# A hybrid decoder block on one Trainium2 core: the order of seven Strassen products, and 512 columns per matmul in two projections

## The chip, the cores and the metric

The kernel runs on one core of one Trainium2 chip. The metric is the device time of one execution in microseconds (us). The kernel before was run three times: 1019.54, 1021.58 and 1021.25 us, median 1021.25.

## The reference

One layer of a decoder with 512 tokens, model width 1024, all in float32:

```
h    = rmsnorm(x, norm_mix_w)
proj = h @ w_in                  # zs, the SSM's inputs, the GDN's inputs, its gate, gs and gg
y    = ssd_scan(...)             # Mamba-2 mixer, 16 heads of 64, 2 groups
y    = y * silu(zs)              # zs: the SSM's gate, 1024 columns
y    = y * rsqrt(mean(y*y) per group of 512) * ssm_norm_w
y_gdn = gated delta rule mixer (8 heads of 128), with its own gate and norm
merged = sigmoid(gs) * (y @ w_proj_ssm) + sigmoid(gg) * (y_gdn @ w_proj_gdn)
x    = x + merged @ w_out        # the output projection
h    = rmsnorm(x, norm_ffn_w)
gate, up = split(h @ w_ffn_in)   # 2 x 2816 columns
x    = x + (silu(gate) * up) @ w_ffn_down
out  = rmsnorm(x, final_norm_w)
```

## The kernel before

Every large product is done as three matmuls (`three`, L342): each float32 operand is split into a high half, rounded to `fp32r`, and a low half, the rest, also `fp32r`; then high by high, high by low and low by high are added in PSUM. `split` (L265) has ScalarE copy the high half (`whi`) and VectorE subtract it from the source for the low half (`wlo`).

**Weights** come in *units* of 128 partitions x 1024 numbers: SP's queue loads one into a buffer `wst`, ScalarE and VectorE split it into `whi` and `wlo` (three buffers each). `cols` (L338) makes of 1024 x 256 weights two units, each of four 128-row tiles by 256 columns. All jobs stand in one list, and their units in one stream. `unit()` (L331) hands the next unit to a job; `ahead(n_split, n_load)` (L278) splits the next units before they are needed, as many as it is told, and loads some more.

**Order.** The program writes the instructions of TensorE (PE), VectorE (DVE) and ScalarE (ACT) in the order in which each engine then runs them. A planner (`Weave`) makes that order: side work, such as a norm after a product, stands in generators, and `tick()` (L85) sets in, between matmuls, what would be ready by the planner's own costs. `start` (L82) begins such work, and `until` (L104) advances the planner's clock until named events are done.

**Jobs around the change**, with the time at which the profiled execution is there: three of the four `gs` jobs (until 503), four `zs` jobs of 256 columns (L1083, 503 to 551), the last `gs` job (to 563), the SSM projection (`ps_job`, to 607), the output projection (`wo_job`, `wo_last`, to 656), the feed-forward blocks (to 894), and the down projection. The last `gs` job stands behind the zs jobs to give the norm after them time.

`gemm_tm` (L377) makes token-major products: for each of four groups of 128 tokens, the activations are the stationary operand and 256 weight columns stream. It goes over the tokens with the first unit, then with the second, and after each token of the second starts `after(t, ...)`. For the zs jobs this is the gate: Silu on ScalarE out of PSUM (`zs`), the product with the scan's output on VectorE (`xg`), and once a group's 512 columns are there, `ssd_norm` (L1066): a square with a sum on ScalarE (`jk`), small steps on GpSimd, a scaling on VectorE, four transposes on TensorE, and their copy and split (`ysh`, `ysl`).

For the output projection `after` is `wo_residual` (L1140): VectorE adds the residual (`x2`), and after a token's last 256 columns come the square on ScalarE (`hn`), two scalings of 512 columns on VectorE (`hn`), eight transposes, copies, and after every second token the split of the transposed activations `h2w` (`h2_split`, L1155; `h2_sums`, L1161). `wo_job` does the first and second 256 columns, `wo_last` (L1201) the third and fourth, two tokens at a time.

**Feed-forward.** The 2816 hidden columns are taken in 11 blocks of 256 for gate and up. The first (`ffn_first`, L1384) is done plainly, with units `wkeep`. The ten others (`ffn_block`, L1399) use Strassen's scheme: seven products instead of eight of 24 matmuls of 256 columns, on sums of the activations and sums of the weights (b11, b21, t1, t2, t3, b22 and b21 once more as a sum). t1 and t3 are summed by a load with addition on GpSimd's queue; t2 and the second b21 by VectorE (`sums` in `ffn_units`, L1272). Seven products write five PSUM banks: P1 and P2 share A, P7 and P4 share C:

```
ORDER = ("P1", "P2", "P5", "P6", "P7", "P3", "P4")                                          # L1265
BANK = {"P1": "A", "P2": "A", "P5": "D", "P6": "B", "P7": "C", "P3": "F", "P4": "C"}         # L1266
until(("a", name), *{"P2": [("p1", fp)], "P4": [("c22", fp)]}.get(name, []))               # L1403
```

P2 adds onto P1 in bank A, and ScalarE's copy `p1` must take P1 out first; P4 adds onto P7 in bank C, and VectorE's `c22` must read it first. `ffn_post` (L1313) is the work on the banks: the copy `p1`, Silu, `u2`, `w`, `c22` and so on. In the last block VectorE and ScalarE also split the activations for the down projection (`actw`, `act_split`, L1416).

Of the kernel before, what the change touches and what calls it, by code (L numbers as in the profile page):

```python
# [14 lines left out]
P = 128  # L15
T = 512
NT = T // P
# [159 lines left out]
def hybrid_block_kernel(  # L177
# [25 lines left out]
    def psum(s="p"):  # L203
        return ps.tile([P, 512], F32, tag="p", name=nm(s))
# [133 lines left out]
    def cols(w, off):  # L338
        return [(w[kh * 512:(kh + 1) * 512, off:off + 256].rearrange("(k p) c -> p k c", p=P), 4, 256)
                for kh in range(2)]  # L340

    def three(p, a, b, first, last, **kw):  # L342

        te.matmul(p, a[0], b[0], start=first, stop=False, **kw)
        te.matmul(p, a[0], b[1], start=False, stop=False, **kw)
        te.matmul(p, a[1], b[0], start=False, stop=last, **kw)
# [29 lines left out]

    def gemm_tm(hT, tokens, after):  # L377

        hhi, hlo = hT
        out_ = {t: psum("pt")[:, 0:256] for t in tokens}  # L380
        for kh in range(2):
            whi, wlo = unit()
            for t in tokens:
                ts = slice(t * P, (t + 1) * P)
                for kk in range(4):
                    k = 4 * kh + kk
                    three(out_[t], (hhi(k)[:, ts], hlo(k)[:, ts]), (whi[:, kk], wlo[:, kk]),
                          k == 0, k == KT - 1)
                    if kk % 2:
                        tick()  # L390
                if kh:
                    start(after(t, out_[t]))
                if t == tokens[0]:
                    ahead(2, 3)


# [685 lines left out]

    def zs_job(g, q):  # L1083
        if g == 0 and q == 0:
            until(("scan", 0), ("scan", 1))
            mid.bcs = m4([D], s="bcs")
            sy.dma_start(mid.bcs, ssm_norm_w.broadcast_to([P, D]))
            mid.ys = (alloc(2, "ysh"), alloc(2, "ysl"))

        def gate(t, p):  # L1090
            zs = s2([256], "zs")
            ac.activation(zs, p, AF.Silu)
            yield HOP
            yv = xg[g][:, t, 256 * q:256 * q + 256]
            ve.tensor_tensor(yv, yv, zs, ALU.mult)
            if q:
                yield from ssd_norm(g, t)

        gemm_tm(hT, range(NT), gate)

# [31 lines left out]
    for g in range(2):  # L1132
        for q in range(2):
            job(lambda g=g, q=q: zs_job(g, q), *cols(w_in, OFF_ZS + 512 * g + 256 * q))
    job(lambda: gs_job(3), *cols(w_in, OFF_GS + 768))
# [4 lines left out]
    def wo_residual(q, t, p):  # L1140
        xv = mid.x2[t // 2][:, t % 2]
        xq = xv[:, 256 * q:256 * q + 256]
        ve.tensor_tensor(xq, p, xq, ALU.add)
        if q == 3:
            hn = b8([D], s="hn")
            yield from norm_T("h2", t, xv, hn, [mid.bcf[:, 0:512], mid.bcf[:, 512:D]], hn, put_h2(t))
            if t % 2:
                spawn(h2_sums(t // 2), wv.cur)
        yield True
# [40 lines left out]
    def wo_job(q):  # L1190
        if q == 0:
# [6 lines left out]
            until(*[("mg", k) for k in range(KT)])  # L1198
        gemm_tm(parts(*mid.mg), range(NT), lambda t, p: wo_residual(q, t, p))

    def wo_last():  # L1201

        mhi, mlo = parts(*mid.mg)

        def piece(p, t, kh, w):
            ts = slice(t * P, (t + 1) * P)
            for kk in range(4):
                k = 4 * kh + kk
                three(p, (mhi(k)[:, ts], mlo(k)[:, ts]), (w[0][:, kk], w[1][:, kk]), k == 0, k == KT - 1)
                if kk % 2:  # L1210
                    tick()

        pts = [psum("pt")[:, 0:256] for _ in range(NT)]
        w = unit()
        for t in range(NT):
            piece(pts[t], t, 0, w)
            if t == 0:
                ahead(2, 3)
        ahead(2, 3)
        ws = []  # L1220

        def second(t):
            if t == 0:
                ws.append(unit())
            piece(pts[t], t, 1, ws[0])
            start(wo_residual(2, t, pts[t]))

        def third(t):
            p = psum("pt")[:, 0:256]
            for kh in range(2):  # L1230
                if t == 0:
                    ws.append(unit())
                piece(p, t, kh, ws[1 + kh])
                if t == NT - 1 and kh == 0:
                    ahead(2, 3)
            start(wo_residual(3, t, p))

        for t in range(2):
            second(t)
            third(t)  # L1240
        second(2)
        second(3)
        ahead(1, 3)
        third(2)
        third(3)

    for q in range(2):
        job(lambda q=q: wo_job(q), *cols(w_out, 256 * q))
    job(wo_last, *cols(w_out, 512), *cols(w_out, 768))

# [13 lines left out]
    NB = FH // 256  # L1264
    ORDER = ("P1", "P2", "P5", "P6", "P7", "P3", "P4")  # L1265
    BANK = {"P1": "A", "P2": "A", "P5": "D", "P6": "B", "P7": "C", "P3": "F", "P4": "C"}  # L1266
# [5 lines left out]
    def ffn_units(fp):  # L1272
# [27 lines left out]
        def sums():  # L1300
# [4 lines left out]
            (lambda: get("b11", 0, 0), None),  # L1305
            (lambda: get("b21", 1, 0), None),
            (t1, sums),
            (t2, None),
# [229 lines left out]
```

## Time and profile before

| | |
|---|---|
| times of three runs | 1019.54, 1021.58, 1021.25 us (median 1021.25) |
| profiled execution, and its span in the trace | 1021.12 us, 1019.4 us |
| instructions | 15625 |
| TensorE matmuls / weight loads | busy 996.5 / 885.7 us, 6394 each |
| VectorE, ScalarE, GpSimd | busy 630.2, 455.3, 96.1 us |
| HBM | 111 GB/s over the span |

The span is the time from the first to the last instruction that the profiler saw; the rest of the execution's time lies around it. A matmul's record ends after the next one has begun, so that a matmul's cost is read from the distance of two starts. In rows of a timeline the columns are the start and the duration in us, engine, line, operation, output <- inputs, shapes, and how many neighbours are joined; in brackets stand the engine's idle time before the row and what ended it. L164, L168 and L153 are lines of helpers that issue every instruction of an engine, so the tiles' names tell the work: `pw`, `pt`, `pdn` are PSUM tiles, `h2w` the split activations of the feed-forward.

### The profile page before, as it was taken

Reading aid. Unit: us, or ns where it says so; the run is one execution under the profiler, and the core shown is the slowest. Engines: PE = TensorE matmul, PEld = TensorE weight load, DVE = VectorE, ACT = ScalarE, POOL = GpSimd, SP = SyncE. Lnnn points to the kernel's source line nnn. Section 1 sums busy time; section 2 is a strip of 40 time slices with the busy share of each in tenths; the row PEclk is TensorE's granted clock in tenths of the full one; section 3 lists DMA queues with packets and bytes.
Section 4 is the critical chain, followed back from the end, with each engine's and each line's share of the span. In section 5 each row is a group of like instructions: output and inputs, shape, how many; then the busy total and the mean of one; then the engine's idle time right before and its main releaser. Section 6 shows DMA issues by size and latency. Waiting matters only on the chain. (4 is left out here: it accounts for less than half of the span.)

```text
span 1019.4 us, 15625 instructions
## 1 busy us (share of the span) xinstructions
PE 996.5 (98%) x6394; PEld 885.7 (87%) x6394; DVE 630.2 (62%) x914; ACT 455.3 (45%) x831; POOL 96.1 (9%) x124
## 2 busy tenths in 40 slices
PE   7999999999999999999999999999999999999997
PEld 5888878888888888878899889999999999988885
DVE  5676699654576879763145463587777777961422
ACT  5466535467676573112345232554344444642222
POOL 2051001100011030000011000111111111000000
PEclk9999999999999999999999999999999999999999
DMA  6242222221112723243332353267677676333322
GB/s 196 63 168 82 83 84 62 64 83 42 42 51 75 248 82 107 80 112 95 104 84 80 107 166 104 62 166 166 166 174 198 158 173 166 108 120 104 99 67 82
DMA packets 99911, 114.02 MB, mean 112 GB/s; under 512 B 6218, under 2 KB 91367, under 8 KB 99072
## 3 DMA queue, kind: packets, MB, share of 16 engines
q1 hardware_dynamic: 89278, 102.54, 32.5%
q0 software_dynamic: 10560, 10.49, 6.8%
q8 instruction: 50, 0.82, 0.3%
q14 instruction: 21, 0.17, 0.1%
q10 hardware_dynamic: 2, 0.00, 0.0%
HBM read 110.87 MB, written 2.15 MB: 111 GB/s over the span
## 5 line engine op out<-in xcount | busy, mean ns | idle before, releaser
L153 DVE TENSOR_TENSOR wlo<-wst,whi 128x1024 fp32r<-128x1024 f32 x174 | 215.0, 1236 | 224.7 <-ACT whi L153 218.5
L153 ACT CAST whi<-wst 128x1024 fp32r<-128x1024 f32 x174 | 182.1, 1048 | 231.4 <-PE pw L164 125.8
L164 PE MATMUL pw<-h2w,whi 128*128 128x256 f32 x1120 | 203.0, 284 | 7.0 <-ACT p L153 7.0
L164 PE MATMUL pw<-hhi,whi 128*128 128x512 f32 (+1 forms) x496 | 196.7, 397 | 0.8 <-ACT whi L153 0.8
L164 PE MATMUL pw<-hhi,wlo 128*128 128x512 f32 (+1 forms) x496 | 191.1, 385 | 2.3 <-DVE wlo L153 2.3
L164 PE MATMUL pw<-hlo,whi 128*128 128x512 f32 (+1 forms) x496 | 190.6, 384 | 0.0
L164 PEld LDWEIGHTS pw<-h2w,whi 128*128 128x128 f32 x1120 | 174.6, 192 | 9.0 <-ACT p L153 9.0
L164 PE MATMUL pw<-h2w,wlo 128*128 128x256 f32 x560 | 158.4, 283 | 0.0
L164 PEld LDWEIGHTS pw<-hhi,wlo 128*128 128x128 f32 x496 | 93.7, 189 | 21.8 <-DVE wlo L153 2.9
L164 PEld LDWEIGHTS pw<-hhi,whi 128*128 128x128 f32 x496 | 93.8, 189 | 17.4 <-ACT whi L153 1.1
L164 PE MATMUL pdn<-whi,actw 128*128 128x512 f32 x352 | 108.6, 389 | 0.0
L164 PEld LDWEIGHTS pw<-hlo,whi 128*128 128x128 f32 x496 | 94.0, 190 | 16.3
L164 PEld LDWEIGHTS pw<-h2w,wlo 128*128 128x128 f32 x560 | 107.5, 192 | 0.0
L164 PEld LDWEIGHTS pdn<-whi,actw 128*128 128x128 f32 x352 | 66.1, 188 | 13.6
L164 PE MATMUL pdn<-wlo,actw 128*128 128x512 f32 x176 | 68.5, 389 | 0.0
L153 DVE SCALAR_TENSOR_TENSOR acc<-pw,pg,acc 128x511 f32<-128x511 f32 (+2 forms) x72 | 53.6, 746 | 2.8 <-ACT acc L153 0.9
L153 POOL DMA_DIRECT2D wst<-in_w_ffn_in_dram x20 | 25.9, 1296 | 243.0 <-DMA wst<-in_w_ffn_in_dram 143.3
L164 PE MATMUL pw<-yg,whi 128*128 128x512 f32 x128 | 42.9, 416 | 0.0
L164 PEld LDWEIGHTS pdn<-wlo,actw 128*128 128x128 f32 x176 | 33.0, 188 | 6.9
L164 PE MATMUL pt<-whi,hhi 128*128 128x256 f32 x128 | 36.5, 285 | 0.0
L164 PE MATMUL pt<-wlo,mgh 128*128 128x256 f32 x128 | 36.3, 284 | 0.1
L164 PE MATMUL pt<-whi,mgh 128*128 128x256 f32 x128 | 36.4, 284 | 0.0
(269 smaller groups left out, 1545.5 us busy)
## 6 DMA issues: line engine op xcount, KB each, us to landing
wst<-in_w_in_dram SPq DMA_DIRECT2D x68, 512.0 KB, 3.7
wst<-in_w_ffn_in_dram SPq DMA_DIRECT2D x54, 512.0 KB, 3.6
wst<-in_w_ffn_down_dram SPq DMA_DIRECT2D x22, 512.0 KB, 3.7
wst<-in_w_ffn_in_dram POOLq DMA_DIRECT2D x20, 512.0 KB, 7.0
decay<-gcd SPq DMA_DIRECT2D x6, 1024.0 KB, 4.3
wst<-in_w_proj_gdn_dram SPq DMA_DIRECT2D x8, 512.0 KB, 3.5
wst<-in_w_proj_ssm_dram SPq DMA_DIRECT2D x8, 512.0 KB, 3.4
wst<-in_w_out_dram SPq DMA_DIRECT2D x8, 512.0 KB, 3.5
```

The source lines that it names most:

```text
L153: return f(out_, *args, **kw)
L164: return self.eng.matmul(out_, lhsT, rhs, **kw)
```

## The change

Three things change. The fifth product runs between the first two, and with it the units' order (t1 before b21) and the place at which `sums` is called. `zs` jobs take 512 columns per matmul instead of 256, one job per group. The output projection becomes two jobs of 512 columns. For both, `wide` makes a unit of two 128-row tiles by 512 columns, and `gemm_tm` goes over the tokens with the first units, and takes the last `late` units token by token; `wo_last` goes.

```diff
@@ -338,6 +338,10 @@
     def cols(w, off):
         return [(w[kh * 512:(kh + 1) * 512, off:off + 256].rearrange("(k p) c -> p k c", p=P), 4, 256)
                 for kh in range(2)]
+
+    def wide(w, off):
+        return [(w[kq * 256:(kq + 1) * 256, off:off + 512].rearrange("(k p) c -> p k c", p=P), 2, 512)
+                for kq in range(4)]
     def three(p, a, b, first, last, **kw):
@@ -374,24 +378,33 @@
                     if kh and ts.stop == T:
                         start(after(j, out_[j]))
-    def gemm_tm(hT, tokens, after):
+    def gemm_tm(hT, after, late=1):
+
         hhi, hlo = hT
-        out_ = {t: psum("pt")[:, 0:256] for t in tokens}
-        for kh in range(2):
-            whi, wlo = unit()
-            for t in tokens:
-                ts = slice(t * P, (t + 1) * P)
-                for kk in range(4):
-                    k = 4 * kh + kk
-                    three(out_[t], (hhi(k)[:, ts], hlo(k)[:, ts]), (whi[:, kk], wlo[:, kk]),
-                          k == 0, k == KT - 1)
-                    if kk % 2:
-                        tick()
-                if kh:
-                    start(after(t, out_[t]))
-                if t == tokens[0]:
+        out_ = [psum("pt") for _ in range(NT)]
+
+        def piece(t, kq, w):
+            ts = slice(t * P, (t + 1) * P)
+            for kk in range(2):
+                k = 2 * kq + kk
+                three(out_[t], (hhi(k)[:, ts], hlo(k)[:, ts]), (w[0][:, kk], w[1][:, kk]),
+                      k == 0, k == KT - 1)
+                tick()
+
+        for kq in range(4 - late):
+            w = unit()
+            for t in range(NT):
+                piece(t, kq, w)
+                if t == 0:
                     ahead(2, 3)
+        ws = [unit() for _ in range(late)]
+        for t in range(NT):
+            for i in range(late):
+                piece(t, 4 - late + i, ws[i])
+                if t == 0 and late == 1 or t == NT - 1 and i < late - 1:
+                    ahead(min(2, i + 1), 3)
+            start(after(t, out_[t]))
     def rsqrt_mean(dst, ss, n, scale):
@@ -1080,23 +1093,21 @@
               pt.rearrange("p (k c) -> p k c", k=4))
         finish(("ys", g, t))
-    def zs_job(g, q):
-        if g == 0 and q == 0:
+    def zs_job(g):
+        if g == 0:
             until(("scan", 0), ("scan", 1))
             mid.bcs = m4([D], s="bcs")
             sy.dma_start(mid.bcs, ssm_norm_w.broadcast_to([P, D]))
             mid.ys = (alloc(2, "ysh"), alloc(2, "ysl"))
         def gate(t, p):
-            zs = s2([256], "zs")
+            zs = s2([512], "zs")
             ac.activation(zs, p, AF.Silu)
             yield HOP
-            yv = xg[g][:, t, 256 * q:256 * q + 256]
-            ve.tensor_tensor(yv, yv, zs, ALU.mult)
-            if q:
-                yield from ssd_norm(g, t)
-
-        gemm_tm(hT, range(NT), gate)
+            ve.tensor_tensor(xg[g][:, t], xg[g][:, t], zs, ALU.mult)
+            yield from ssd_norm(g, t)
+
+        gemm_tm(hT, gate)
     def gs_job(q):
@@ -1130,8 +1141,7 @@
     for q in range(3):
         job(lambda q=q: gs_job(q), *cols(w_in, OFF_GS + 256 * q))
     for g in range(2):
-        for q in range(2):
-            job(lambda g=g, q=q: zs_job(g, q), *cols(w_in, OFF_ZS + 512 * g + 256 * q))
+        job(lambda g=g: zs_job(g), *wide(w_in, OFF_ZS + 512 * g))
     job(lambda: gs_job(3), *cols(w_in, OFF_GS + 768))
     for q in range(4):
         job(lambda q=q: ps_job(q), *cols(w_proj_ssm, 256 * q))
@@ -1139,9 +1149,9 @@
     def wo_residual(q, t, p):
         xv = mid.x2[t // 2][:, t % 2]
-        xq = xv[:, 256 * q:256 * q + 256]
+        xq = xv[:, 512 * q:512 * q + 512]
         ve.tensor_tensor(xq, p, xq, ALU.add)
-        if q == 3:
+        if q == 1:
             hn = b8([D], s="hn")
             yield from norm_T("h2", t, xv, hn, [mid.bcf[:, 0:512], mid.bcf[:, 512:D]], hn, put_h2(t))
             if t % 2:
@@ -1196,57 +1206,10 @@
             sy.dma_start(mid.bcf, norm_ffn_w.broadcast_to([P, D]))
             mid.hq = [b8([2, 4, 256], F32, "hq") for _ in range(2)]
             until(*[("mg", k) for k in range(KT)])
-        gemm_tm(parts(*mid.mg), range(NT), lambda t, p: wo_residual(q, t, p))
-
-    def wo_last():
-
...
-        def second(t):
-            if t == 0:
-                ws.append(unit())
-            piece(pts[t], t, 1, ws[0])
-            start(wo_residual(2, t, pts[t]))
-
-        def third(t):
-            p = psum("pt")[:, 0:256]
-            for kh in range(2):
-                if t == 0:
-                    ws.append(unit())
-                piece(p, t, kh, ws[1 + kh])
-                if t == NT - 1 and kh == 0:
-                    ahead(2, 3)
-            start(wo_residual(3, t, p))
-
-        for t in range(2):
-            second(t)
-            third(t)
-        second(2)
-        second(3)
-        ahead(1, 3)
-        third(2)
-        third(3)
+        gemm_tm(parts(*mid.mg), lambda t, p: wo_residual(q, t, p), 3 if q else 1)
     for q in range(2):
-        job(lambda q=q: wo_job(q), *cols(w_out, 256 * q))
-    job(wo_last, *cols(w_out, 512), *cols(w_out, 768))
+        job(lambda q=q: wo_job(q), *wide(w_out, 512 * q))
@@ -1262,7 +1225,7 @@
     ffn.a = {}
     ffn.act = []
     NB = FH // 256
-    ORDER = ("P1", "P2", "P5", "P6", "P7", "P3", "P4")
+    ORDER = ("P1", "P5", "P2", "P6", "P7", "P3", "P4")
     BANK = {"P1": "A", "P2": "A", "P5": "D", "P6": "B", "P7": "C", "P3": "F", "P4": "C"}
     def ffn_src(r, c, fp):
@@ -1303,8 +1266,8 @@
         return [(Source(g, p), 4, 256) for g, p in (
             (lambda: get("b11", 0, 0), None),
-            (lambda: get("b21", 1, 0), None),
-            (t1, sums),
+            (t1, None),
+            (lambda: get("b21", 1, 0), sums),
             (t2, None),
             (t3, None),
             (lambda: w.b22, None),
```

The order of the instructions moves with it. On ScalarE, between the gates of the second SSM group and the last `gs` job: `whi` is a weight unit's high half, `zs` the gate, `jk` the square, `ysh` the copy of the transposed result. Before:

```order
L153 CAST whi_724_4827<-wst_690_4587 128x1024
L153 ACTIVATE zs_727_4881<-pt_720_4810 128x256
L153 CAST whi_728_4883<-wst_708_4675 128x1024
L153 ACTIVATE jk_731_4896,ss_732_4897<-xg_500_3229 128x512
L153 ACTIVATE zs_733_4905<-pt_721_4811 128x256
L153 ACTIVATE jk_734_4922,ss_735_4923<-xg_500_3229 128x512
L153 ACTIVATE zs_736_4925<-pt_722_4812 128x256
L153 ACTIVATE zs_737_4942<-pt_723_4813 128x256
L153 ACTIVATE jk_740_4953,ss_741_4954<-xg_500_3229 128x512
L153 ACTIVATE jk_742_4957,ss_743_4958<-xg_500_3229 128x512
L153 CAST ysh_663_4384<-pyt_744_4969 128x4x128
L153 CAST whi_745_4980<-wst_715_4756 128x1024
```

and now:

```order
L153 CAST whi_708_4645<-wst_698_4559 128x1024
L153 ACTIVATE zs_711_4675<-pt_689_4531 128x512
L153 ACTIVATE jk_712_4681,ss_713_4682<-xg_500_3229 128x512
L153 ACTIVATE zs_714_4689<-pt_690_4532 128x512
L153 ACTIVATE jk_715_4695,ss_716_4696<-xg_500_3229 128x512
L153 ACTIVATE zs_717_4704<-pt_691_4533 128x512
L153 ACTIVATE jk_718_4710,ss_719_4711<-xg_500_3229 128x512
L153 ACTIVATE zs_720_4717<-pt_692_4534 128x512
L153 CAST ysh_663_4384<-pyt_723_4727 128x4x128
L153 ACTIVATE jk_724_4737,ss_725_4738<-xg_500_3229 128x512
L153 CAST ysh_663_4384<-pyt_726_4747 128x4x128
L153 CAST whi_727_4754<-wst_701_4565 128x1024
```

Before, both units of the last `gs` job (`whi_724`, `whi_728`) stand ahead of most of the norm; now the first (`whi_708`) does, and the second (`whi_727`) stands behind all four squares.

On VectorE, from the output projection to the first feed-forward block: `x2` is the residual, `hn` the scaling, `wkeep` the low half of the first feed-forward block's units, `h2w` of its activations. Before:

```order
L153 TENSOR_TENSOR x2_791_5334<-pt_817_5579,x2_791_5334 128x256
L153 TENSOR_TENSOR x2_791_5334<-pt_818_5580,x2_791_5334 128x256
L153 TENSOR_TENSOR wkeep_834_5781<-wst_814_5536,wkeep_834_5781 128x1024
L153 TENSOR_TENSOR h2w_838_5801<-hq_793_5341,h2w_838_5801 128x1024
L153 TENSOR_TENSOR h2w_839_5816<-hq_793_5341,h2w_839_5816 128x1024
L153 TENSOR_TENSOR x2_791_5334<-pt_837_5788,x2_791_5334 128x256
L153 TENSOR_TENSOR wkeep_843_5836<-wst_821_5597,wkeep_843_5836 128x1024
L153 TENSOR_TENSOR x2_791_5334<-pt_842_5823,x2_791_5334 128x256
L153 TENSOR_TENSOR wkeep_849_5873<-wst_835_5784,wkeep_849_5873 128x1024
L153 SCALAR_TENSOR_TENSOR hn_840_5820<-x2_791_5334,ss_841_5821,bcf_792_5339 128x512 x2
L153 SCALAR_TENSOR_TENSOR hn_845_5854<-x2_791_5334,ss_846_5855,bcf_792_5339 128x512 x2
L153 TENSOR_TENSOR wkeep_851_5908<-wst_836_5786,wkeep_851_5908 128x1024
```

and now:

```order
L153 TENSOR_TENSOR x2_775_5110<-pt_794_5245,x2_775_5110 128x512
L153 TENSOR_TENSOR h2w_814_5388<-hq_777_5117,h2w_814_5388 128x1024
L153 SCALAR_TENSOR_TENSOR hn_812_5382<-x2_775_5110,ss_813_5383,bcf_776_5115 128x512 x2
L153 TENSOR_TENSOR wkeep_815_5398<-wst_798_5257,wkeep_815_5398 128x1024
L153 TENSOR_TENSOR wkeep_818_5411<-wst_801_5263,wkeep_818_5411 128x1024
L153 TENSOR_TENSOR h2w_820_5419<-hq_777_5117,h2w_820_5419 128x1024
L153 TENSOR_TENSOR x2_775_5110<-pt_795_5246,x2_775_5110 128x512
L153 SCALAR_TENSOR_TENSOR hn_821_5426<-x2_775_5110,ss_822_5427,bcf_776_5115 128x512 x2
L153 TENSOR_TENSOR wkeep_827_5459<-wst_816_5401,wkeep_827_5459 128x1024
L153 TENSOR_TENSOR h2w_831_5501<-hq_778_5118,h2w_831_5501 128x1024
L153 TENSOR_TENSOR wkeep_832_5504<-wst_817_5403,wkeep_832_5504 128x1024
L153 TENSOR_TENSOR h2w_834_5515<-hq_778_5118,h2w_834_5515 128x1024
```

The first low half of weights (`wkeep_815`) now stands behind the scaling of the third token group (`hn_812`) and behind a low half of activations (`h2w_814`), and the last residual (`x2_775` from `pt_795`) behind two more.

On VectorE, in the last feed-forward block: `u2`, `w` and `c22` read banks, `wlo` and `actw` are low halves. Before:

```order
L153 TENSOR_TENSOR u2_1158_8353<-pw_1152_8312,p1_1144_8247 128x512
L153 TENSOR_TENSOR w_1159_8354<-pw_1147_8277,u2_1158_8353 128x512
L153 TENSOR_TENSOR actw_1160_8357<-act_903_6365,actw_1160_8357 128x1024
L153 TENSOR_TENSOR wlo_1162_8367<-wst_1123_8092,whi_1161_8366 128x1024
L153 TENSOR_TENSOR c22_1165_8391<-w_1159_8354,pw_1157_8346 128x512
L153 TENSOR_TENSOR wlo_1167_8400<-wst_1151_8298,whi_1166_8399 128x1024
```

and now:

```order
L153 TENSOR_TENSOR u2_1134_7921<-pw_1127_7876,p1_1121_7822 128x512
L153 TENSOR_TENSOR w_1135_7922<-pw_1119_7812,u2_1134_7921 128x512
L153 TENSOR_TENSOR wlo_1137_7932<-wst_1105_7696,whi_1136_7931 128x1024
L153 TENSOR_TENSOR actw_1140_7956<-act_879_5933,actw_1140_7956 128x1024
L153 TENSOR_TENSOR wlo_1142_7966<-wst_1126_7862,whi_1141_7965 128x1024
L153 TENSOR_TENSOR c22_1144_7977<-w_1135_7922,pw_1132_7911 128x512
```

`c22` now stands behind three low halves after `w`, where it stood behind two.

## Rows read from the trace of the kernel before

**Rows 1.** the page's busy line: busy us, share of the span, instructions
```profile
PE 996.5 (98%) x6394; PEld 885.7 (87%) x6394; DVE 630.2 (62%) x914; ACT 455.3 (45%) x831; POOL 96.1 (9%) x124
```

**Rows 2.** TensorE's waits: us in all, times, longest us
```profile
PE pw L164 <- ACT p L153: 7.0, 10, 0.9
```

**Rows 3.** timeline, TensorE, between the first two products of an ordinary block
```profile
768.51 0.28 PE L164 MATMUL pw<-h2w,wlo 128*128 128x256 f32 x1
769.47 0.50 PE L164 MATMUL pw<-h2w,whi 128*128 128x256 f32 x2 [0.68 <-ACT p L153]
```

**Rows 4.** the same view and seam, last feed-forward block
```profile
873.97 0.28 PE L164 MATMUL pw<-h2w,wlo 128*128 128x256 f32 x1
875.19 0.50 PE L164 MATMUL pw<-h2w,whi 128*128 128x256 f32 x2 [0.94 <-ACT p L153]
```

**Rows 5.** timeline, TensorE, zs gate: 37 starts, first and last
```profile
544.75 0.28 PE L164 MATMUL pt<-whi,hhi 128*128 128x256 f32 x1
...
549.07 0.28 PE L164 MATMUL pt<-whi,hhi 128*128 128x256 f32 x1
```

**Rows 6.** timeline, TensorE, 512-column matmuls: 57 starts, first and last
```profile
484.71 0.39 PE L164 MATMUL pw<-hhi,whi 128*128 128x512 f32 x1
...
497.40 0.39 PE L164 MATMUL pw<-hhi,wlo 128*128 128x512 f32 x1
```

**Rows 7.** windows, down projection: busy us (instructions) per engine, clock, DMA share, GB/s
```profile
915.00:965.00 50.00, 50.00 (x222) 41.41 (x221) 17.12 (x22) 12.77 (x18) 0.00 (x0) 1.00 0.32 95
```

**Rows 8.** timeline, ScalarE, the Silu after P2 in the last block
```profile
878.36 0.60 ACT L153 ACTIVATE act<-pw 128x512 f32<-128x512 f32 x1 [1.11 <-PE pw L164]
```

**Rows 9.** timeline, VectorE, last block, around the same time
```profile
874.89 1.22 DVE L153 TENSOR_TENSOR t<-wst,wst 128x1024 f32<-128x1024 f32 x1
...
877.28 1.22 DVE L153 TENSOR_TENSOR actw<-act,actw 128x1024 fp32r<-128x1024 f32 x1
878.42 1.22 DVE L153 TENSOR_TENSOR wlo<-t,whi 128x1024 fp32r<-128x1024 f32 x1
```

**Rows 10.** timeline, ScalarE and VectorE, end of the last zs job
```profile
549.81 0.63 ACT L153 ACTIVATE jk<-xg 128x512 f32<-128x512 f32 x1 [1.69 <-DVE xg L153]
...
550.44 0.36 ACT L153 ACTIVATE zs<-pt 128x256 f32<-128x256 f32 x1
...
550.84 0.43 DVE L153 TENSOR_TENSOR xg<-xg,zs 128x256 f32<-128x256 f32 x1 [1.12 <-ACT zs L153]
...
551.36 0.63 ACT L153 ACTIVATE jk<-xg 128x512 f32<-128x512 f32 x1 [0.55 <-DVE xg L153]
```

**Rows 11.** groups by shape: busy us, mean ns, idle before them and its releaser
```profile
L153 ACT CAST whi<-wst 128x1024 fp32r<-128x1024 f32 x174 | 182.1, 1048 | 231.4 <-PE pw L164 125.8 <-PE pdn L164 63.4 <-issue 23.3
...
L153 DVE TENSOR_TENSOR act<-w,act 128x512 f32<-128x512 f32 x10 | 6.9, 693 | 0.3
```

**Rows 12.** timeline, ScalarE and VectorE, output projection
```profile
641.31 1.06 ACT L153 ACTIVATE hn<-x 128x1024 f32<-128x1024 f32 x1 [4.15 <-DVE x L153]
...
643.40 1.42 DVE L153 SCALAR_TENSOR_TENSOR hn<-x,ss,bcf 128x512 f32<-128x512 f32 x2 [2.19 <-POOL ss L153]
...
651.44 1.23 DVE L153 TENSOR_TENSOR wkeep<-wst,wkeep 128x1024 fp32r<-128x1024 f32 x1 [1.65 <-ACT wkeep L153]
```

**Rows 13.** timeline, TensorE, output projection
```profile
638.79 0.28 PE L164 MATMUL pt<-whi,mgh 128*128 128x256 f32 x1
639.17 0.39 PE L164 MATMUL pt<-wlo,mgh 128*128 128x256 f32 x1
...
645.63 1.04 PE L168 MATMUL pt<-ident,hn 128*128 128x128 f32 x8
```

**Rows 14.** timeline, TensorE, first feed-forward block (a row joins neighbours of one form)
```profile
658.07 1.19 PE L164 MATMUL pw<-h2w,wkeep 128*128 128x256 f32 x6
...
661.13 0.76 PE L164 MATMUL pw<-h2w,wkeep 128*128 128x256 f32 x5
...
662.51 0.62 PE L164 MATMUL pw<-h2w,wkeep 128*128 128x256 f32 x3 [0.62 <-DVE wkeep L153]
```

More of the change, by code (lines that the diff above doesn't have):

```diff
@@ L1198, in wo_job @@
             until(*[("mg", k) for k in range(KT)])
-        gemm_tm(parts(*mid.mg), range(NT), lambda t, p: wo_residual(q, t, p))
-    def wo_last():
[L1203 to L1216, printed above, removed]
-            if t == 0:
-                ahead(2, 3)
-        ahead(2, 3)
-        ws = []
-        def second(t):
-            if t == 0:
-                ws.append(unit())
-            piece(pts[t], t, 1, ws[0])
-            start(wo_residual(2, t, pts[t]))
-        def third(t):
-            p = psum("pt")[:, 0:256]
-            for kh in range(2):
-                if t == 0:
-                    ws.append(unit())
-                piece(p, t, kh, ws[1 + kh])
-                if t == NT - 1 and kh == 0:
-                    ahead(2, 3)
-            start(wo_residual(3, t, p))
-        for t in range(2):
-            second(t)
-            third(t)
-        second(2)
-        second(3)
-        ahead(1, 3)
-        third(2)
-        third(3)
+        gemm_tm(parts(*mid.mg), lambda t, p: wo_residual(q, t, p), 3 if q else 1)
     for q in range(2):
-        job(lambda q=q: wo_job(q), *cols(w_out, 256 * q))
-    job(wo_last, *cols(w_out, 512), *cols(w_out, 768))
+        job(lambda q=q: wo_job(q), *wide(w_out, 512 * q))
     ffn = Batch()
```

## The prediction

> **What bounds the kernel now.** I read the page's busy line first, then TensorE's waits, then the timeline around each wait. The busy line has TensorE's matmuls at 98% of the span, and no other engine above 62% [rows 1]. So the time is the number of matmuls times their spacing, plus the places where TensorE stands still. The list of waits names one place above all: ten waits on ScalarE's copy `p` [rows 2]. In the timeline this is the seam between the feed-forward block's first two products: the last matmul of P1 starts at 768.51 and the first of P2 at 769.47, because both write bank A and P1 must be copied out first [rows 3]. The usual step there is 0.12, so 0.84 is lost, and the two matmuls after it take 0.50 where such a pair takes 0.40: 0.10 more. 0.94 per block; in the last block the gap is 1.22, so 1.10 + 0.10 = 1.20 [rows 4].
>
> **Width.** A matmul of 256 columns starts 0.1200 after the one before (36 steps from 544.75 to 549.07) [rows 5]; one of 512 columns 0.2266 after (56 steps from 484.71 to 497.40) [rows 6]. The down projection, which has the very operand order of the new form (activations stationary, weights streaming, 512 columns), does 222 in 50.00 us, 0.225 each [rows 7]. Two narrow ones cost 0.2400, one wide one 0.2266: 13.4 ns saved per pair. Both jobs together have 2 x 384 narrow matmuls, which become 384 wide ones: 384 x 13.4 ns = **-5.1**. Bytes and splits stay: every weight tile still has 1024 columns per partition, and SP's queue issues the same loads in the same order.
>
> On this a rule of the Trainium skill speaks against the change ("TensorE: Matmul & The Clock Gate", section "Back-to-back issue gap": the gap is N/2.4 + 2.5 ns, so the fixed part is 2.5 ns per matmul). By it 384 pairs would give 1.0 us, not 5.1; the rows do not agree, since their fixed part is 13.4.
>
> **The seam.** P5 between P1 and P2 gives the copy a whole product, 24 x 0.12 = 2.88, and it takes 0.6 (what ScalarE needs for 512 columns out of PSUM [rows 8]). Nine blocks give back 9 x 0.94 = 8.46, the last 1.20: **-9.7**. What is late next in an ordinary block? The third matmul of P6 (the first that reads the low half of t2), at 24 x 0.12 x 3 + 0.24 = 8.88 after P1's first. In the last block P1's first matmul starts 23 x 0.12 before its last, 873.97 - 2.76 = 871.21; the low half starts at 878.42, 7.21 later, and takes 1.22 [rows 4, 9]. An ordinary block has one activation split less ahead of it (1.14, from 877.28 to 878.42), so 7.3 against 8.88: hidden, with 1.6 to spare. P5's weight sum is needed one product earlier; SP and POOL issue it in the same order as before, so I cost it at nothing, and at 2.88 in one block if its second half lands late in the first.
>
> **Where waits are added.** The new token-major routine splits only one unit ahead in its last pass where the old one split two, and the planner now puts weight splits behind the norm chain. ScalarE and VectorE work strictly in the printed order, so I walk four places with durations of before. Restarting after a wait costs 0.10, as above.
>
> *First to second zs job.* Count from the start of the first job's last pass. A token takes 6 x 0.2266 = 1.36; its gate can start at 1.55 (a wide matmul's row lasts 0.39). From square to square, a token took 1.55 on ScalarE [rows 10]; the gate goes from 0.36 to 0.60 and the product from 0.43 to 0.69 [rows 8, 10, 11], so 2.05. The fourth gate starts at 7.7 and ends at 8.3. Behind it stand token 0's transposed copy (0.6), then token 3's square, which waits for VectorE's low part (0.69) and product (0.69): it starts at 10.1. Only then comes the second unit's split: high half 10.75 to 11.8 (1.05 [rows 11]), low half 11.85 to 13.05 (1.23 [rows 12]). TensorE gets there at 5.44 + 5.44 + three groups of four transposes of 0.11 (eight take 1.04, the last one's run included [rows 13]) = 12.2 and reads the low half with its second matmul, at 12.43. It waits 0.65 + 0.10 = **+0.75**.
>
> *Second zs job to the last gs job.* The same count, with one copy more ahead (0.5): high half done at 12.3, low half at 13.55. TensorE needs the low half with the third matmul, 12.2 + 0.45: **+1.03**.
>
> *Output projection to the feed-forward.* Count from token 0's last three quarters (18 x 0.2266 = 4.08 per token; tokens 0 and 1's 16 transposes, 1.78, fall into token 2). Token 2 ends at 13.98, token 3 at 18.06. Token 2's residual (0.69) starts at 14.2, its square at 14.95; behind it ScalarE has one h2 split (16.0), then the first weight split (16.95 to 18.0). VectorE does the h2 low half (17.1), two scalings (18.2 to 19.55, 1.42 the pair [rows 12]), and only then the weights' low half, 19.55 to 20.78. TensorE needs it with its third matmul at 18.30: 2.5 + 0.10. Token 3 is worse off: its residual stands behind two more splits (1.14 each), 23.0; square at 23.75; from square to scaling took 2.09 before (641.31 to 643.40) [rows 12], so the scaled halves end at 26.6 and 27.26. TensorE is at their transposes at 24.46 and waits 2.2, then 0.2. Together **+5.0**. What goes there: 638.79 to 639.17 and its follow-on, 0.26 + 0.10 [rows 13]; the six matmuls from 658.07, 1.19 where 5 x 0.12 + 0.28 = 0.88 would do, 0.31; and the five from 661.13 after which the next came at 662.51 instead of 661.73, 0.78 + 0.10 [rows 14]. **-1.55**.
>
> *Last block.* VectorE also splits the activations here. The copy of bank C (`c22`), for which P4 waits, now stands behind one more weight split. From 7.21 (low half of t2) on: t3's low half 8.35; the Silu after P2 starts 3.07 after P2's first matmul (878.36 less 875.19, less the restart) [rows 4, 8], so at 8.83, and the activation split's high half ends at 10.36. Then low halves on VectorE every 1.14 (`actw`, b22, `actw`): 10.4, 11.5, 12.7; u2 13.8, w 14.5, b21 15.1, `actw` 16.25, down's first unit 17.4, c22 18.5 to 19.2. P4 could start at 144 x 0.12 = 17.28: 1.95 + 0.10 = **+2.05**. That is a wait which the old seam hid.
>
> **Sum.** Against the profiled execution, 1021.12 (span 1019.4 and 1.7 around it; the median of the runs is 0.13 above): -5.1 - 9.7 + 0.75 + 1.03 + 5.0 - 1.55 + 2.05 = -7.5, so **1013.6**. Bounds: with none of the four places waiting, 1021.1 - 5.1 - 9.7 - 1.55 = 1004.8. With one more high and low half (1.05 + 1.23) ahead of each of the four, +9.1: 1022.7. I take the walked values, since each is an order in print with durations of the same instructions; what can be off is a start by a few tenths at each place.
>
> **Rivals.**
> - *The places do not wait* (chance 0.12). TensorE may reach the joints later than I count, or a scaling may be done sooner; before, with the same chains, it lost only 1.55 at the output joint. For it: VectorE was idle 2.2 before such scalings [rows 12]. Against it: the order is fixed. Half of the added waits gone: 1013.6 - 4.4 = 1009.2; all gone, 1004.8.
> - *The joints take more* (0.07). Each a half more than counted, +4.4: 1018.0.
> - *The seam only moves* (0.05). If P2 waits after P5 for b21's split as long as it waited for the copy, 9.7 stays: 1023.3 less what P5's start gains, some 2: about 1021. Against it: before, b21's split was done before t1's, and SP's order is unchanged.
> - *Wide matmuls give nothing* (0.03): if the 13.4 ns hang on streaming weights and not on the instruction, -5.1 goes: 1018.7. Rows 7 speak against it. The Trainium skill's formula, named above, would leave 1.0 of the 5.1: an estimate of 1017.7.
> - *Slower* (0.04): the weight sums slip in every block. They run on VectorE ahead of t2's low half, and P6 now comes 0.94 sooner. The 1.6 of slack go first; with three instructions of 1.14 more ahead (one low half and the two steps of a sum) a block loses 3.4 - 1.6 = 1.8, and 0.1 for the restart: 10 x 1.9 = 19 gives 1032.6. From 1.6 + 0.75 = 2.35 on the change loses. Speaking against: VectorE ran these instructions without a gap from 874.89 on [rows 9], so nothing is left to be pushed in but work that the order shows.
>
> **Chances.** Forecast 0.69, with its own range 1011 to 1017; rivals 0.12, 0.07, 0.05, 0.03, 0.04. What this measurement can tell from no change is about 0.2%, 2 us, so 1019.2 and 1023.3 are the limits. Faster: 0.69 + 0.12 + 0.07 + 0.03, less 0.01 = 0.90. Same: 0.06 (the moved seam and the edge of its neighbours). Slower: 0.04. The range for 8 in 10 reaches into the first two rivals: 1009 to 1017.5.
>
> **What would show it.** Right: no gap of 0.94 between the first two products of a block; block period 7 x 2.88 = 20.16; 384 wide `pt` matmuls at 0.227; waits of TensorE on the low halves `wlo` at two places around 510 to 555, on `wkeep` and `hn` of 2 to 3 us after the output projection, and one of 2 on `c` in the last block. Wrong: a block period above 20.2, or a wide `pt` spacing near 0.24, or no wait at the joints (then the time is below 1009).

## The result and the profile after

The changed kernel took 1014.90 us (median of four runs, 1014.37 to 1015.61), the kernel before 1020.75 in the same set: a ratio of 0.9944, 95% interval 0.9928 to 0.9960. A second set gave 0.9937 (0.9923 to 0.9951). The forecast was 1013.6.

The page's busy line, to be held against [rows 1], has 384 matmuls less and a span of 1013.9 us:

```profile
PE 991.6 (98%) x6010; PEld 866.1 (85%) x6010; DVE 628.4 (62%) x898; ACT 454.0 (45%) x823; POOL 94.9 (9%) x124
```

TensorE's list of waits (us in all, times, longest). The ten waits on `p` of [rows 2] are gone from it; `hn`, a long one on `wkeep` and a wait put down to `actw` are new:

```profile
PE pw L164 <- DVE wlo L153: 2.9, 3, 2.1
PE pt L168 <- DVE hn L153: 2.1, 1, 2.1
PE pw L164 <- DVE wkeep L153: 2.1, 1, 2.1
PE pw L164 <- ACT actw L153: 1.9, 1, 1.9
PE pw L164 <- ACT whi L153: 0.8, 2, 0.6
```

Whole executions hide where time went, since what stands ahead of the zs jobs, which no edit touched, ended between 500.76 and 503.71 in the profiles of this study. So I cut every profile at the same matmuls: the first of the zs jobs, of the SSM projection, of the output projection, of the first Strassen block and of the down projection. All rows below are distances between such starts, in us; the SSM projection (43.52), the down projection (119.85 to 119.89) and what follows it (6.97 to 7.00) are the same in all and left out.

| profile | ahead of zs | zs and last gs | output projection and first block | ten Strassen blocks | span |
|---|---|---|---|---|---|
| before | 503.07 | 60.53 | 74.26 | 211.18 | 1019.4 |
| after | 503.13 | 59.97 | 76.68 | 203.75 | 1013.9 |
| after, second set | 500.76 | 59.95 | 75.25 | 203.75 | 1010.1 |
| p5_only | 503.71 | 60.53 | 74.25 | 205.25 | 1014.1 |
| zs_only | 500.83 | 59.93 | 74.26 | 211.19 | 1016.6 |
| wo_only | 502.54 | 60.53 | 75.25 | 211.19 | 1019.9 |
| wk_t2 | 502.79 | 59.97 | 72.99 | 203.75 | 1009.9 |
| hn_late | 502.19 | 59.97 | 75.38 | 205.25 | 1013.1 |
| wk_hn | 502.32 | 59.97 | 72.13 | 203.76 | 1008.5 |
| late1_2 | 502.18 | 58.17 | 75.26 | 203.76 | 1009.7 |
| c22_1 | 501.62 | 59.92 | 75.26 | 201.60 | 1008.8 |
| all_four | 501.75 | 58.17 | 72.12 | 201.60 | 1004.0 |
| all_five | 502.44 | 58.17 | 71.39 | 201.60 | 1004.0 |
| p5_zs_fix | 502.11 | 58.17 | 74.26 | 201.60 | 1006.5 |

The span fell by 5.5: 7.43 in the Strassen blocks and 0.56 in the zs jobs, less 2.42 that the output projection's stretch gave back.

*The seam.* Windows from the first matmul of one Strassen block to that of the next, two blocks of the changed kernel (busy us and instructions of PE, PEld, DVE, ACT, POOL, then the granted clock, DMA share, GB/s). A block is seven products of 2.88 without a gap, where [rows 3] had 0.94 more:

```profile
683.30:703.46 20.16, 20.16 (x171) 20.16 (x169) 14.63 (x15) 8.92 (x10) 1.27 (x1) 1.00 0.47 112
703.46:723.62 20.16, 20.16 (x171) 20.16 (x169) 15.43 (x16) 8.84 (x10) 2.57 (x2) 1.00 0.75 184
```

*The last block.* TensorE's timeline, where the gap of [rows 4] stood between P1 and P2. It is now ahead of P4, 2.21 from start to start:

```profile
881.90 0.28 PE L164 MATMUL pw<-h2w,wlo 128*128 128x256 f32 x1
884.11 0.48 PE L164 MATMUL pw<-h2w,whi 128*128 128x256 f32 x2 [1.94 <-ACT actw L153]
```

The bracket names `actw`, which P4 does not read. VectorE's timeline shows what does end there: the copy of bank C (`c`) behind three low halves, done at 883.96:

```profile
879.27 0.69 DVE L153 TENSOR_TENSOR w<-pw,u 128x512 f32<-128x512 f32 x1
879.88 1.22 DVE L153 TENSOR_TENSOR wlo<-wst,whi 128x1024 fp32r<-128x1024 f32 x1
881.01 1.22 DVE L153 TENSOR_TENSOR actw<-act,actw 128x1024 fp32r<-128x1024 f32 x1
882.15 1.22 DVE L153 TENSOR_TENSOR wlo<-wst,whi 128x1024 fp32r<-128x1024 f32 x1
883.28 0.68 DVE L153 TENSOR_TENSOR c<-w,pw 128x512 f32<-128x512 f32 x1
```

*The zs joints.* TensorE's timeline after the first and after the second zs job. At the second, the matmul at 556.24 starts once ScalarE's high half has come, the one at 557.50 once VectorE's low half has:

```profile
531.63 0.48 PE L164 MATMUL pt<-whi,hhi 128*128 128x512 f32 x1
532.33 0.50 PE L164 MATMUL pt<-wlo,hhi 128*128 128x512 f32 x1 [0.22 <-DVE wlo L153]
...
555.46 0.60 PE L168 MATMUL pyt<-ident,xg 128*128 128x128 f32 x4
556.24 0.50 PE L164 MATMUL pw<-hhi,whi 128*128 128x512 f32 x1 [0.19 <-ACT whi L153]
556.59 0.39 PE L164 MATMUL pw<-hlo,whi 128*128 128x512 f32 x1
557.50 0.50 PE L164 MATMUL pw<-hhi,wlo 128*128 128x512 f32 x1 [0.53 <-DVE wlo L153]
```

*The output joint*, where [rows 13, 14] had their small gaps: TensorE's timeline has two standstills, and the eight transposes after the second take 1.75 where [rows 13] had 1.04:

```profile
651.97 0.66 PE L164 MATMUL pw<-h2w,wkeep 128*128 128x256 f32 x2
654.71 0.74 PE L164 MATMUL pw<-h2w,wkeep 128*128 128x256 f32 x4 [2.08 <-DVE wkeep L153]
655.29 1.04 PE L168 MATMUL pt<-ident,hn 128*128 128x128 f32 x8
656.08 2.40 PE L164 MATMUL pw<-h2w,wkeep 128*128 128x256 f32 x18
660.61 1.75 PE L168 MATMUL pt<-ident,hn 128*128 128x128 f32 x8 [2.13 <-DVE hn L153]
```

The windows of the same stretch say why. The number behind POOL's is the granted clock: 0.55 from 660.60 to 664.30, so for most of it the lower of the two levels, 1.2 GHz, after TensorE had been busy 0.73 of 2.80 us, then 3.49 of 3.50, then 0.28 of 2.40:

```profile
651.90:654.70 2.80, 0.73 (x4) 0.37 (x2) 2.80 (x5) 1.88 (x2) 0.00 (x0) 1.00 0.00 0
654.70:658.20 3.50, 3.49 (x30) 3.49 (x30) 2.83 (x3) 0.59 (x1) 0.00 (x0) 1.00 0.62 172
658.20:660.60 2.40, 0.28 (x3) 0.10 (x2) 0.89 (x2) 2.40 (x5) 0.74 (x2) 1.00 0.56 186
660.60:664.30 3.70, 3.69 (x19) 3.46 (x20) 2.00 (x3) 2.56 (x5) 0.00 (x0) 0.55 0.19 50
664.30:668.00 3.70, 3.70 (x32) 3.70 (x32) 3.70 (x4) 3.67 (x5) 0.00 (x0) 0.99 0.34 114
```

### The profile page after: what moved, and what is told of

Read it like the earlier page. It is cut to its first block, busy times and chain, and to the rows that moved or that the text cites. A ratio compares the mean times of both kernels' runs of the same rounds, so it can differ in the third digit from the quotient of the medians.

```text
span 1013.9 us, 14829 instructions
## 1 busy us (share of the span) xinstructions
PE 991.6 (98%) x6010; PEld 866.1 (85%) x6010; DVE 628.4 (62%) x898; ACT 454.0 (45%) x823; POOL 94.9 (9%) x124
## 3 DMA queue, kind: packets, MB, share of 16 engines
HBM read 110.87 MB, written 2.15 MB: 111 GB/s over the span
## 5 line engine op out<-in xcount | busy, mean ns | idle before, releaser
L164 PEld LDWEIGHTS pw<-yg,whi 128*128 128x128 f32 x128 | 24.0, 188 | 8.2 <-issue 3.6
L153 DVE SCALAR_TENSOR_TENSOR acc<-pw,pss,acc 128x511 f32<-128x511 f32 (+2 forms) x36 | 26.7, 747 | 1.8 <-ACT acc L153 0.9
L164 PE MATMUL pw<-h2w,wkeep 128*128 128x256 f32 x192 | 25.3, 293 | 2.1 <-DVE wkeep L153 2.1
```

The lines of the kernel that those rows point to most:

```text
L153: return f(out_, *args, **kw)
L164: return self.eng.matmul(out_, lhsT, rhs, **kw)
```

## The experiments

The first question was whether the parts add, and which of them pays. Each ratio is against the kernel before as it ran in the same set, with a median of 1020.80, 1019.86 or 1019.98 us; so times of different sets are compared by their ratios or by the stages of the table.

**p5_only**: the kernel before, with the new order alone.

```diff
-    ORDER = ("P1", "P2", "P5", "P6", "P7", "P3", "P4")
+    ORDER = ("P1", "P5", "P2", "P6", "P7", "P3", "P4")
...
-            (lambda: get("b21", 1, 0), None),
-            (t1, sums),
+            (t1, None),
+            (lambda: get("b21", 1, 0), sums),
```

> Only the fifth product moves between the first two; both projections keep 256 columns. Theory (the parts add, each with the time of its own stage): the ten Strassen blocks, which took 211.18 us before and 203.75 after, carry -7.43; so 1020.75 - 7.4 = 1013.3, faster than the whole change (1014.9). The new wait before P4 in the last block (2.2 us) is there here too. Rival (the parts work on each other: the order gains only with the joint that the wide matmuls give): less than 5.8 gained, over 1015. Second rival: the wait before P4 comes from the planner's other shifts and is absent: 1011.1.

1013.71 us, ratio 0.9935 (0.9921 to 0.9950). Within the intervals the order alone gives what the whole change gives. Its other stages stand as before; its blocks took 205.25, not 203.75: the wait before P4 is there (2.22), and behind it TensorE runs at the lower clock, 0.60 over 882.80 to 887.00, which accounts for the 1.50.

**zs_only** and **wo_only**: the kernel before, with one projection each at 512 columns. Of each edit only the jobs' lines are shown; `wide`, the new token-major routine beside the old one, and the gate or the residual go with them as in the change.

```diff
-        for q in range(2):
-            job(lambda g=g, q=q: zs_job(g, q), *cols(w_in, OFF_ZS + 512 * g + 256 * q))
+        job(lambda g=g: zs_job(g), *wide(w_in, OFF_ZS + 512 * g))
...
```

> Only the zs gate gets 512 columns per matmul. Theory: its stage with the last gs job took 60.53 us before and 59.97 after, so -0.56: 1020.2, no difference that can be told from none; TensorE waits some 0.5 and some 1.1 us on weight splits at the two joints. Rival (a wide matmul gives nothing, the waits only cost): +1.9, 1022.6.

1019.95 us, ratio 0.9996 (0.9988 to 1.0005), no difference; 59.93 for 60.53 in its stage.

```diff
-        job(lambda q=q: wo_job(q), *cols(w_out, 256 * q))
-    job(wo_last, *cols(w_out, 512), *cols(w_out, 768))
+        job(lambda q=q: wo_job(q), *wide(w_out, 512 * q))
...
```

> Only the output projection gets 512 columns per matmul. Theory: the stretch from its first matmul to the end of the first feed-forward block took 74.26 us before and 76.68 after, so +2.42: 1023.2, slower than before: the part loses by itself. Rival (the half clock after its two waits was chance in one profile): +0.9, 1021.7. Second rival (the width gives 2.6 and the waits come from elsewhere): -2.6, 1018.2.

1021.50 us, ratio 1.0009 (1.0000 to 1.0018). Its stretch took 75.25: 0.99 more than before, not 2.42. Both standstills are there (2.46 and 2.42 from start to start), but no stretch at the lower clock follows, so 1.43 of the profile's 2.42 was that. Here the first rival was right. By its stage the part as changed is a small loss; the whole time's interval just reaches no difference.

The next runs take away one wait each from the changed kernel.

**wk_t2**: the feed-forward's first units split earlier.

```diff
-                if t == 0 and late == 1 or t == NT - 1 and i < late - 1:
+                if t == 0 and late == 1 or t == NT - 2 and i < late - 1:
```

> The changed kernel, but the first two weight units of the first feed-forward block are split during the third token group of the output projection instead of the fourth, ahead of that group's residual. Both theories: the wait on wkeep (2.34, with its surroundings 2.6) goes; the wait on hn for the fourth group's transposes stays, 2.2 to 2.7. Theory A: the half clock that follows costs 1.5 because TensorE stood still twice within 8 us; with one standstill it goes too: -4.1, 1010.8. Theory B: the second standstill alone brings it: -2.6, 1012.3.

1011.04 us, ratio 0.9908 (0.9895 to 0.9921). The stretch took 72.99, which is 2.26 less than 75.25: the wait on `wkeep` is gone, one of 0.97 on the low half of the first split activations (`h2w`) shows in its place, and the wait on `hn` fell to 1.64. No lower clock. That speaks for A or B alike, since neither standstill at this joint is over 2 us any more.

**hn_late**: the fourth group's transposes later.

```diff
             ve.scalar_tensor_tensor(dst[:, hs], xv[:, hs], ss, bc[h], ALU.mult, ALU.mult)
+        if event == "h2" and t == NT - 1:
+            wv.cur += 3000.0
```

> The changed kernel, with the transposes of the fourth token group in the output projection's norm written 30 matmuls later on TensorE. Both theories: the wait on hn (2.29) goes, since those 30 matmuls last 3.6; the wait on wkeep stays (2.6). Theory A (half clock only after two standstills close together): it goes as well, 1014.9 - 2.3 - 1.45 = 1011.2. Theory B (any standstill of over 2 us can bring it, in some executions): 1012.6 where it keeps coming, and rows with a granted clock of 0.5 after 654.7 in some profiles. Rival (the third product then waits for the activations that come later): 1014.9.

1013.89 us, ratio 0.9940 (0.9928 to 0.9952). The wait on `hn` is gone. In part the rival came true: a wait of 1.08 on later activations. The stretch took 75.38: 75.25 less 2.29 plus 1.08, and 1.34 more. Windows of this kernel, at the output joint and at the last block, show where that comes from, and the 1.50 in the Strassen blocks: after a single standstill each, the clock is at 0.52 and at 0.54. So theory A, two standstills close together, falls:

```profile
651.00:653.70 2.70, 0.69 (x3) 0.36 (x2) 2.70 (x5) 1.83 (x2) 0.00 (x0) 1.00 0.00 0
653.70:657.10 3.40, 3.34 (x15) 3.34 (x16) 2.88 (x4) 0.44 (x1) 0.00 (x0) 0.52 0.62 175
...
879.60:882.20 2.60, 0.67 (x6) 0.49 (x6) 2.60 (x4) 2.25 (x3) 0.00 (x0) 1.00 0.60 202
882.20:885.80 3.60, 3.60 (x21) 3.60 (x20) 3.56 (x5) 0.00 (x0) 0.00 (x0) 0.54 0.47 145
```

**wk_hn**: the edits of wk_t2 and hn_late together.

> Both moves at once: the first two weight units of the feed-forward split during the third token group, and the fourth group's transposes later. The stretch from the output projection's first matmul to the end of the first feed-forward block took 76.68 in the changed kernel, 72.99 with the early split alone; the wait on hn (1.64) and its follow-on (0.2) go from that: 71.15, and one wait of 0.97 on the split activations stays. 1014.9 - 5.5 = 1009.4. No stretch at half clock there. Rival (waits move on to the third product): 1011.0.

1010.48 us, ratio 0.9913 (0.9899 to 0.9926); 72.13 in the stretch, not 71.15. TensorE's timeline shows the wait that I expected, and one that only the rival had, on the third product: it needs the third unit's low half, which stands behind the last group's scaling on VectorE.

```profile
652.15 1.58 PE L164 MATMUL pw<-h2w,wkeep 128*128 128x256 f32 x11 [0.71 <-DVE h2w L153]
...
659.94 0.39 PE L164 MATMUL pw<-h2w,wkeep 128*128 128x256 f32 x1 [0.79 <-DVE wkeep L153]
```

**late1_2**: two units split ahead in the zs jobs' last pass.

```diff
-                    ahead(min(2, i + 1), 3)
+                    ahead(2 if late == 1 else i + 1, 3)
```

> The changed kernel, but in the last pass of the zs jobs two units are split ahead instead of one, ahead of the gates. Theory: the standstills at the two joints (0.59 and 1.27 in the profile) go: 1014.9 - 1.86 = 1013.0. Rival (the gates and squares come later by that split, and the SSM projection then waits for the norm): no gain, 1014.9; the wait then stands on ysh or ysl at the projection's start.

1011.69 us, ratio 0.9924 (0.9912 to 0.9937). The stage took 58.17 for 59.97, so the joints cost 1.80, and nothing came back in the SSM projection. (Here the lower clock followed the first standstill at the output joint. TensorE came later to the wait on `hn` by what that cost, and the wait was shorter for it: the stretch took 75.26 all the same.)

**c22_1**: most activation splits of the last block behind `c22`.

```diff
-            yield [("ffn", fp), ("P", NB - 1, ORDER[max(0, (fp + 1) // 2 - 1)])]
+            yield [("ffn", fp), ("P", NB - 1, ORDER[max(0, (fp + 1) // 2 - 1)])] + ([("c22", NB - 1)] if fp > 1 else [])
```

> The changed kernel, but in the last Strassen block nine of the eleven activation splits for the down projection are put behind the copy of bank C. Theory: the wait before P4 (2.10, follow-on 0.07) goes: 1014.9 - 2.2 = 1012.7, and a half-clock stretch behind it, where an execution has one, goes too (up to 1.5 more). Rival (the splits are then late for the down projection): a wait of 1 to 3 on actw in its first pieces, 1014 or more.

1011.38 us, ratio 0.9924 (0.9910 to 0.9937). The blocks took 201.60, ten times 20.16, and the down projection 119.87: no wait took its place. VectorE's timeline has the copy behind one low half now:

```profile
875.16 0.69 DVE L153 TENSOR_TENSOR w<-pw,u 128x512 f32<-128x512 f32 x1
875.77 1.22 DVE L153 TENSOR_TENSOR wlo<-wst,whi 128x1024 fp32r<-128x1024 f32 x1
876.90 0.68 DVE L153 TENSOR_TENSOR c<-w,pw 128x512 f32<-128x512 f32 x1
```

The last four runs: the moves together, and the changed kernel once more.

**all_four** (wk_hn, late1_2 and c22_1 together), and **all_five**, which splits a third unit before the last residual:

> The four moves together on the changed kernel: weight units split earlier at the output projection, its last transposes later, two units split ahead in the zs jobs, and the activation splits of the last block behind the copy of bank C. Theory (stages add): against the kernel before, zs and last gs job 58.17 for 60.53, output projection with the first block 72.13 for 74.26, Strassen blocks 201.60 for 211.18: -14.1, which is 0.986 of before. Rival (moves disturb each other, or the time returns in the SSM projection or down projection): 0.990 or more.

```diff
+                elif late > 1 and t == NT - 1 and i == 0:
+                    ahead(3, 3)
```

> As all_four, and a third weight unit of the first feed-forward block is split before the last token group's residual. Theory: the wait of 0.95 with its 0.10 before that block's third product goes: -15.1, which is 0.985 of before. Rival (the split in front of the residual delays the transposes as much): as all_four.

1006.39 us, ratio 0.9867 (0.9851 to 0.9883), and 1005.37 us, ratio 0.9854 (0.9840 to 0.9868). The stages add: 14.1 less than before in all_four by the table, as expected, and 14.8 in all_five, where 15.1 was expected; the third unit gave 0.73 by its stage, not 1.05, and the intervals of the two whole times overlap. In all_five's timeline the second standstill of wk_hn is gone from the output joint:

```profile
649.49 0.28 PE L164 MATMUL pw<-h2w,wkeep 128*128 128x256 f32 x1
650.47 1.58 PE L164 MATMUL pw<-h2w,wkeep 128*128 128x256 f32 x11 [0.71 <-DVE h2w L153]
651.89 1.04 PE L168 MATMUL pt<-ident,hn 128*128 128x128 f32 x8
652.68 5.99 PE L164 MATMUL pw<-h2w,wkeep 128*128 128x256 f32 x48
```

**p5_zs_fix**: p5_only and zs_only together, with the edits of late1_2 and c22_1; the output projection as before.

> The fifth product between the first two, the zs gate with 512 columns and two units split ahead, the activation splits behind the copy of bank C, and the output projection as before, with 256 columns. Theory: 58.17 for 60.53, 74.26 as before, 201.60 for 211.18: -11.9, which is 0.988 of before; so the wide output projection is worth 2.1 to 3.2 once its joint is mended, and was a loss of 1.0 without. Rival (the width of the output projection gives nothing even then): the same as all_four.

1008.94 us, ratio 0.9895 (0.9881 to 0.9909). Its output stretch is that of before, 74.26, against 71.39 in all_five: the wide output projection is worth 2.87 with its joint mended. Not all of that is width. If a pair saves there what it saves in the zs jobs, the width gives 2.36, and the rest is old gaps that went with it; whether the same moves would close those gaps with 256 columns too was not run.

**after_again**: the changed kernel, nothing edited.

> The changed kernel once more, beside the others on the same chip. Theory B of the half clock (a standstill of over 2 us can bring some 3.5 us at half clock, in some executions, not in others): the stage times are those of the first profile but for one: the stretch of the output projection with the first block is 75.3 without such a spell or 76.7 with one, and the Strassen blocks 203.75 or 205.25. Theory C (it belongs to this kernel's second standstill): 76.7 and 203.75 again.

1014.44 us, and in its profile, of an execution of 1011.78, all three standstills with the clock at 1.00 behind each: 75.25 and 203.75. So the lower clock belongs to no one place of this kernel (C falls); what decides whether a standstill brings it stays open.

## Why the prediction was right, and where it was off

| term | forecast | measured | from |
|---|---|---|---|
| width, zs jobs (half of -5.1) | -2.6 | -2.36 | late1_2 less before |
| zs joints | +0.75, +1.03 | +1.80 | after less late1_2 |
| output projection: width, joint, old gaps (-2.6 + 5.0 - 1.55) | +0.9 | +0.99 | wo_only less before |
| seam | -9.7 | -9.58 | c22_1 less before |
| wait before P4 | +2.05 | +2.15 | after less c22_1 |
| lower clock after a standstill | 0 | +1.43 | after less its second profile |
| ahead of the zs jobs | 0 | +0.06 | profiles |
| sum | -7.5 | -5.5 | |

*The seam* went as forecast, and nothing was late next in an ordinary block: the two windows above hold no gap. The rivals in which the seam moves, or the weight sums slip, are answered by the same rows.

*The width*: 102 wide matmuls of the first zs job took 23.12, 0.2267 each, where the forecast took 0.2266. The stage as a whole shows 2.36 for 192 pairs, 12.3 ns a pair. The Trainium skill ("TensorE: Matmul & The Clock Gate", section "Back-to-back issue gap") has N/2.4 + 2.5 ns, which would have left an estimate of 2.5 ns a pair. The Trainium skill calls this, in the same section, the gap of a single matmul by itself, and says that with a weight load beside each one it counts too little at small N and too much at large N; the prediction used the formula without that. In this kernel, where each matmul brings its own weight load, the formula gives an estimate of 109.2 ns at 256 columns and 215.8 at 512. The rows show steps of 120.0 and 226.7: it counts too little at both widths, so the trace does not bear out that it counts too much at large N.

*The zs joints*: the sum was right, its split less so. At the first TensorE lost 0.48 and a restart of 0.11, at the second 0.35 and 0.69 with two restarts. There the second unit's high half was late too, not its low half alone.

*The output joint*: forecast 2.5 + 0.10 on `wkeep` and 2.2 + 0.2 on `hn`; measured, start to start less the usual step, 2.34 and 2.29, and 0.1 to 0.25 around each. The rival in which the places do not wait is out, and wo_only shows that this part of the change was no gain.

*The last block*: 2.05 forecast, 2.10 + 0.07 measured, and c22_1 shows that it hung on the place of `c22`, as argued.

*What was mis-sized* is the sentence "Restarting after a wait costs 0.10, as above". It was read from standstills of 0.9 to 1.2 us. The change made three of 2.2 to 2.5, and after such a one the clock was at times at its lower level. That is 1.43 of the 2.0 between the forecast of -7.5 and the profile's -5.5; the rest lies in the other rows, none of them off by more than 0.25.

The median of all runs lies 5.85 below before, 1.7 short of the forecast, and the granted clock that is on record for each run points the same way. Of the changed kernel's nine runs two have a mean clock of 0.996 and took 1011.78 and 1012.09; the seven others have 0.992 to 0.994 and took 1014.37 to 1015.61. The kernel before has 0.994 to 0.998, mostly 0.995, in the 23 runs beside p5_only. How much of the lower clock in a run without a profile stands at the joints, and how much ahead of the zs jobs, is not shown.

## What to carry to other kernels

Where one engine is busy 98% of the time and the others run in a written order, walk each joint instruction by instruction with durations from the trace: five such terms came out within 0.25 us here. Price each part of a change apart: of three parts one paid for all, one gave 0.6 and one lost 1.0, until splits and transposes were moved by a few instructions; then the two gave 2.4 and 2.9. A wider step leaves fewer places to put side work in; look at what stands ahead of the first use after it, and at which engine that is queued on.

## What was not expected of the hardware

Nine of the profiles here hold, together, 17 standstills of TensorE of 2.2 to 2.5 us between two starts after the first 470 us. After 5 of them the granted clock fell to the lower level for a stretch, and a stage took 1.4 to 1.5 longer where no later wait took it up; after 12 it stayed at 1.00. The same kernel, run twice, had it after its second standstill of three, and after none. After shorter waits (up to 1.8) none of these profiles shows it there.

It also came without a standstill, ahead of every edit. In seven of the fourteen profiles the clock was lower around 190, in all_five around 251. In the kernel before, it fell behind 96 matmuls of 32x32, from 186.67 on, and four transposes, with TensorE busy throughout:

```profile
186.00:190.00 4.00, 4.00 (x103) 3.57 (x102) 3.38 (x4) 0.49 (x2) 0.00 (x0) 1.00 0.33 84
190.00:193.40 3.40, 3.40 (x11) 2.72 (x10) 0.00 (x0) 3.15 (x12) 0.55 (x2) 0.50 0.18 63
```

zs_only, with the same matmuls in the same order, stayed at 1.00 there.

The time until the first zs matmul, a part that no edit touched, was in the fourteen profiles between 500.76 and 503.71, more than any part but the order was worth. Two things make that scatter. One is this stretch: the 300 matmuls from 187 on took 40.8 us with it and 39.24 without; in all_five it cost as much later. The other is the beginning: the 201st matmul started between 41.57 and 43.60. What lies between and behind repeats to 0.05. Comparing stages between the same matmuls gave differences that repeated to 0.05, which whole times could not.
